# Softmax attention: a scheduling step that issues a transpose of probabilities before the next pair's scores

## The chip, the cores and the metric

The kernel runs on one core of a Trainium2 chip. TensorE multiplies matrices (its matmuls are "PE" in the profile, its weight loads "PEld"). VectorE (DVE) and ScalarE (ACT) do elementwise work, GpSimd (POOL) a few small operations, and SyncE (SP) issues the DMAs. Each engine takes its instructions in the order in which they stand for it, and waits on semaphores for the others. The metric is the device time of one execution in microseconds (us). The kernel before takes 996.15 us in the median of three runs (992.35, 996.15 and 997.11).

## The reference

256 tokens of width 1024 pass a first block (stick-breaking attention, pooling, spatial gating and an MLP), and then a second block of two layers, each with an MLP: a convolution layer, and an attention layer. The change is in the attention layer. The reference writes it as block-sparse attention with blocks of 256 keys; with 256 tokens there is one block, so that what is left is causal softmax attention with a distance penalty, in 16 heads of 64:

```
q, k, v = split(h @ w_qkv, 3)                     # 256 x 1024 each
q = rms_norm(to_heads(q), q_norm_g); k = rms_norm(to_heads(k), k_norm_g); v = to_heads(v)
s = einsum('bhqd,bhkd->bhqk', q, k) / sqrt(64) - slope[h] * (t_q - t_k)   # -inf where t_k > t_q
p = softmax(s, axis=-1)
y = einsum('bhqk,bhkd->bhqd', p, v) merged over heads @ w_o
x = x + g1 * y                                    # and then the MLP of this layer
```

All of it is fp32 to within the tolerance; a matrix product by weights is done in three fp32r products of high and low parts.

## The kernel before, in words

**Weights.** All weights stream through one list of 1 MB halves in the order of their use. A half is loaded by SP into one of three raw buffers, then split into a high part by ACT (`wH`, L352, two instructions a half) and a low part by DVE (`wL`, L353, two instructions), which go into one of four slots. A slot comes free when the product that reads it is done, and the split of a later half waits for that. So each product of the program releases splitting work on ACT and DVE.

**A job.** `ts_job` (L513) multiplies 128 tokens by 512 columns of weights: 24 matmuls of 128x512 (L446 to L448) into one PSUM bank of kind A. The attention layer has eight jobs for queries and keys (two halves `n` of the heads, two token tiles `t`, query and key), four jobs for the values, and four for the output matrix `ao`. Below, Q1 and K1 are the last two query and key jobs (`n`=1, `t`=1), V00, V01, V10, V11 the value jobs (`n`, `t`).

**Queries and keys.** After a query or key job, `qk_norm` (L1193) squares on ACT (L1196), sums by head on DVE (L1197), takes the power -1/2 on POOL (L1198, L1199) and multiplies on DVE (L1201). `qk_trans` (L1205) then transposes the 128x512 result by four PE transposes (L1210) into a bank of kind B, and ACT copies it out (L1211).

**Scores.** `at_scores(h0)` (L1216) handles the two heads h0 and h0+1, named S0, S2, ..., S14 below: matmuls into two B banks (L1224), and then for each head on DVE the penalty added (L1228), two maxima (L1230, L1231), on ACT two exponentials with their sums (L1232, L1233), and on DVE the reciprocal and two multiplications (L1234 to L1236). The probabilities stay in one of four buffers `w15`.

**Transposes of probabilities.** `at_trans(h)` (L1241), named T0 to T15, transposes the three 128x128 blocks of one head by PE into a B bank (L1245), and ACT copies them out (L1250).

**Value products.** `av(h)` (L1287), named W0, W2, ..., W14, multiplies two heads' transposed probabilities by the values (L1295, L1296); every second one splits a bank into the high and low parts that `ao` reads (L500, L501).

**What sets the order.** The program calls `at_step` at fixed places: two calls after each of the last three query and key jobs, three after each value job, then loops until the value products are done. A step issues the scores of a pair when at most two heads have scores that are not transposed yet (`state["s"] - state["t"] <= 2`), and a transpose when more than `AHEAD` = 2 heads are ahead, or when all scores up to the limit are issued. The order of the calls sets priorities. A scheduler then places each engine's instructions by them and by its own estimate of when inputs are ready, so that the order on an engine is near to, and not the same as, the order of the calls. There are four B banks, which scores and both kinds of transposes share.

Of the kernel before, what the change touches and what calls it, by code (L numbers as in the profile page):

```python
# [105 lines left out]
def net_kernel(ctx: ExitStack, tc: tile.TileContext, I, out):  # L106
# [8 lines left out]
    def nm(s):  # L115
        cnt[0] += 1
        return f"{s}_{cnt[0]}"
# [3 lines left out]
    def T(shape, tag, bufs, dt=F32):  # L121
        if tag in BASE_PAD and tag not in based:
            based.add(tag)
            sb.tile([P, BASE_PAD[tag]], F32, tag="pad" + tag, bufs=1, name=nm("pad"))
        return sb.tile(shape, dt, tag=tag, bufs=bufs, name=nm(tag))
# [4 lines left out]
    def bankB():  # L130
        return ps.tile([P, 512], F32, tag="B", name=nm("B"))
# [1084 lines left out]
    def at_scores(h0):  # L1216

        n, c = h0 // 8, (h0 % 8) // 2
        q, k = QK[0, n], QK[1, n]
        zs = [bankB(), bankB()]  # L1220
        for q0, q1, k1 in ((0, P, P), (P, S, S)):
            for i, z in enumerate(zs):
                po = slice(i * 64, i * 64 + 64)
                mm(z[:, q0:q0 + k1], q[po, c, q0:q1], k[po, c, 0:k1], start=True, stop=True)  # L1224
        for i, z in enumerate(zs):
            h = h0 + i
            s = wk.tile([P, 384], F32, tag="w15", bufs=4, name=nm("w15"))
            stt(s, dist, -slopes[h], z[:, :384], op0=ALU.mult, op1=ALU.add)  # L1228
            m = T([P, 2], "ss", 4)
            nc.vector.reduce_max(m[:, 0:1], s[:, 0:P], axis=AX.X, negate=True)  # L1230
            nc.vector.reduce_max(m[:, 1:2], s[:, P:384], axis=AX.X, negate=True)  # L1231
            act(s[:, 0:P], s[:, 0:P], AF.Exp, bias=m[:, 0:1], accum_out=sums[:, 0, h:h + 1])  # L1232
            act(s[:, P:384], s[:, P:384], AF.Exp, bias=m[:, 1:2], accum_out=sums[:, 1, h:h + 1])  # L1233
            nc.vector.reciprocal(sums[:, :, h:h + 1], sums[:, :, h:h + 1])  # L1234
            vts(s[:, 0:P], s[:, 0:P], sums[:, 0, h:h + 1], None, op0=ALU.mult)
            vts(s[:, P:384], s[:, P:384], sums[:, 1, h:h + 1], None, op0=ALU.mult)  # L1236
            stp[h] = s
# [3 lines left out]
    def at_trans(h):  # L1241
        s = stp.pop(h)
        pt = bankB()
        for i in range(3):
            nc.tensor.transpose(pt[:, i * P:(i + 1) * P], s[:, i * P:(i + 1) * P], ident)  # L1245
        if h % 2 == 0:
            tag, bufs = ("q4", 4) if 8 <= h < 12 else ("hidH" if h % 4 else "hidL", 2)
            ptt[h // 2] = T([P, 2, 384], tag, bufs)
        PT[h] = ptt[h // 2][:, h % 2, :]
        act(PT[h], pt[:, :384], AF.Copy)  # L1250

    state = {"s": 0, "t": 0, "o": 0}

    def at_step(lim):
        if state["s"] < lim and state["s"] - state["t"] <= 2:
            at_scores(state["s"])
            state["s"] += 2
        if state["t"] < state["s"] - AHEAD or (state["t"] < state["s"] and state["s"] >= lim):
            if state["t"] < 12 or state["o"] >= state["t"] - 10:
                at_trans(state["t"])  # L1260
                state["t"] += 1

    pend = []

# [4 lines left out]
    for n in range(2):  # L1269
        bq, bk = B["aq", n], B["ak", n]  # L1270
        need(bq, bk)
        for t in range(NT):
            for i, b in enumerate((bq, bk)):
                a = ts_job(hk, t, b)
                qn = qk_norm(a)
                if t == 1:
                    done(b)
                flush(HOLD)
                pend.append((n, t, i, qn))
                if n == 1 and t + i > 0:  # L1280
                    for _ in range(2):
                        at_step(8)
# [22 lines left out]
    for n in range(2):  # L1305
        need(B["av", n])
        for t in range(NT):
            a = ts_job(hk, t, B["av", n])
            if t == 1:
                done(B["av", n])  # L1310
            act(vt[t][:, n * 512:(n + 1) * 512], a, AF.Copy)
            flush()
            for _ in range(3):
                at_step(16)
                if n == 1:
                    av_next(8)
    while state["o"] < 8:
        at_step(16)
        av_next(8)
# [45 lines left out]
```

## Time and profile before

| what | value |
|---|---|
| median of three runs | 996.15 us (992.35 to 997.11) |
| the profiled execution's own time | 997.19 us |
| its span | 995.5 us |
| PE busy | 967.3 us, 97% of the span, 4969 matmuls |
| DVE, ACT, POOL busy | 75%, 57%, 6% |
| granted TensorE clock, mean | 0.997 |
| attention, from the first scores to the start of `ao` | 722.8 to 786.3 us |
| mean DMA rate | 224 GB/s |

An engine is busy while it executes instructions; the ends of matmuls are modelled, so that PE's 97% says where PE had work and not how well it was used. The granted clock is 1.00 at TensorE's full 2.4 GHz and 0.50 at 1.2 GHz. In the timeline, a note in brackets gives the engine's idle time ahead of the instruction and what ended it.

### The profile page before, as it was taken

Reading aid. Unit: us, or ns where it says so; the run is one execution under the profiler, and the core shown is the slowest. Engines: PE = TensorE matmul, PEld = TensorE weight load, DVE = VectorE, ACT = ScalarE, POOL = GpSimd, SP = SyncE. Lnnn points to the kernel's source line nnn. Section 1 sums busy time; section 2 is a strip of 40 time slices with the busy share of each in tenths; the row PEclk is TensorE's granted clock in tenths of the full one; section 3 lists DMA queues with packets and bytes.
Section 4 is the critical chain, followed back from the end, with each engine's and each line's share of the span. In section 5 each row is a group of like instructions: output and inputs, shape, how many; then the busy total and the mean of one; then the engine's idle time right before and its main releaser. Section 6 shows DMA issues by size and latency. Waiting matters only on the chain.

```text
span 995.5 us, 13007 instructions
## 1 busy us (share of the span) xinstructions
PE 967.3 (97%) x4969; PEld 798.1 (80%) x4969; DVE 743.9 (75%) x1036; ACT 564.0 (57%) x872; POOL 59.2 (6%) x84
## 2 busy tenths in 40 slices
PE   7999999988999999999999999999999999999998
PEld 5998889877788887875778888888866778888886
DVE  6858887787587887989788678869578586766553
ACT  5656784456466556523556666555477456656561
POOL 4002010010000000100000000000420000000000
PEclk9999999999999999999999999999999999999999
DMA  7877686577667986678269777865534246567531
GB/s 249 278 275 258 233 285 239 186 248 258 236 224 263 311 297 228 213 266 274 84 217 311 270 258 253 306 247 198 176 121 170 85 143 238 212 241 255 201 128 43
DMA packets 102044, 223.38 MB, mean 224 GB/s; under 512 B 4316, under 2 KB 8310, under 8 KB 101982
## 3 DMA queue, kind: packets, MB, share of 16 engines
q1 hardware_dynamic: 101982, 222.55, 64.8%
q8 instruction: 39, 0.64, 0.3%
q14 instruction: 23, 0.19, 0.1%
HBM read 221.44 MB, written 1.10 MB: 224 GB/s over the span
## 4 chain that ended last, share of the span: by engine, by line
PE 74%; DVE 13%; DMA 4%; ACT 3%; issue 3%; POOL 2%; POOLq 0%; SPq 0%; ACTq 0%; DVEq 0%
PE B L461 14%; PE A L448 12%; PE A L447 12%; PE A L446 12%; PE B L462 7%; DVE wL L353 5%; PE A L461 4%; DMA raw<-in_ada_w_dram 2%; PE A L462 2%; ACT wH L352 2%; DVE acc L372 2%; POOL rst L531 2%; PE A L453 1%; PE A L454 1%; PE A L455 1%
## 5 line engine op out<-in xcount | busy, mean ns | idle before, releaser
L353 DVE TENSOR_TENSOR wL<-raw,wH 128x1024 fp32r<-128x1024 f32 x306 | 361.9, 1220 | 82.6 <-ACT wH L352 81.5
L352 ACT ACTIVATE wH<-raw 128x1024 fp32r<-128x1024 f32 x306 | 307.2, 1050 | 153.5 <-PE A L448 97.4
L461 PE MATMUL B<-hHL,wH 128*128 128x512 f32 x576 | 205.2, 400 | 0.0
L462 PE MATMUL B<-hHL,wL 128*128 128x256 f32 x576 | 162.3, 282 | 0.0
L446 PE MATMUL A<-wH,hidH 128*128 128x512 f32 x384 | 151.3, 394 | 0.0
L447 PE MATMUL A<-wL,hidH 128*128 128x512 f32 x384 | 150.5, 392 | 0.0
L448 PE MATMUL A<-wH,hidL 128*128 128x512 f32 x384 | 150.3, 391 | 0.0
L372 DVE SCALAR_TENSOR_TENSOR acc<-raw,cond,acc 128x512 f32<-128x512 f32 x168 | 125.7, 748 | 13.0 <-DMA raw<-in_ada_w_dram 10.2
L446 PE MATMUL A<-wH,hHL 128*128 128x512 f32 (+1 forms) x336 | 130.4, 388 | 1.5 <-ACT wH L352 0.8
L461 PEld LDWEIGHTS B<-hHL,wH 128*128 128x128 f32 x576 | 109.0, 189 | 26.9
L447 PE MATMUL A<-wL,hHL 128*128 128x512 f32 (+1 forms) x336 | 129.1, 384 | 0.5 <-DVE wL L353 0.5
L448 PE MATMUL A<-wH,hHL 128*128 128x512 f32 (+1 forms) x336 | 128.9, 384 | 0.0
L462 PEld LDWEIGHTS B<-hHL,wL 128*128 128x128 f32 x576 | 109.4, 190 | 0.8
L446 PEld LDWEIGHTS A<-wH,hidH 128*128 128x128 f32 x384 | 72.4, 189 | 16.0 <-issue 0.8
L448 PEld LDWEIGHTS A<-wH,hidL 128*128 128x128 f32 x384 | 72.5, 189 | 15.6
L447 PEld LDWEIGHTS A<-wL,hidH 128*128 128x128 f32 x384 | 72.6, 189 | 14.7
L446 PEld LDWEIGHTS A<-wH,hHL 128*128 128x128 f32 x336 | 63.7, 190 | 15.1 <-issue 1.3
L447 PEld LDWEIGHTS A<-wL,hHL 128*128 128x128 f32 x336 | 63.6, 189 | 13.0 <-DVE wL L353 1.0
L448 PEld LDWEIGHTS A<-wH,hHL 128*128 128x128 f32 x336 | 63.5, 189 | 12.5 <-issue 0.3
L461 PE MATMUL A<-hHL,wH 128*128 128x512 f32 x192 | 68.2, 398 | 0.0
L968 ACT ACTIVATE rs<-B 128x256 f32<-128x256 f32 x72 | 27.1, 376 | 50.5 <-PE B L462 50.4
L531 POOL TENSOR_TENSOR rst<-rst,neghalf 128x1 f32<-128x1 f32 x20 | 18.4, 923 | 625.5 <-DVE rst L528 560.8
(242 smaller groups left out, 1269.2 us busy)
## 6 DMA issues: line engine op xcount, KB each, us to landing
raw<-in_mlp_w_dram SPq DMA_DIRECT2D x64, 1024.0 KB
raw<-in_ada_w_dram SPq DMA_DIRECT2D x48, 1024.0 KB
raw<-in_w_in_dram SPq DMA_DIRECT2D x19, 1024.0 KB
raw<-in_w_ff_in_dram SPq DMA_DIRECT2D x16, 1024.0 KB
raw<-in_w_ff_out_dram SPq DMA_DIRECT2D x16, 1024.0 KB
raw<-in_attn_w_qkv_dram SPq DMA_DIRECT2D x12, 1024.0 KB
raw<-in_conv_w_in_dram SPq DMA_DIRECT2D x8, 1024.0 KB
ada<-mod SPq DMA_DIRECT2D x24, 256.0 KB
```

Of the source, the lines that this page charges most:

```text
L352: act(h[:, p:q, :], v[:, p:q, :], AF.Copy)
L353: nc.vector.tensor_sub(l[:, p:q, :], v[:, p:q, :], h[:, p:q, :].bitcast(F32))
L372: stt(acc_cur[0], v[:, c, :], cond[:, k:k + 1], src, op0=ALU.mult, op1=ALU.add)
L446: mm(dst, lh(xc), wh, start=s0, stop=False)
L447: mm(dst, lh(xc), wl, start=False, stop=False)
L448: mm(dst, ll(xc), wh, start=False, stop=s1)
L453: mm(dst, wh, rh(xc), start=(i == 0), stop=False)
L454: mm(dst, wh, rl(xc), start=False, stop=False)
L461: mm(dst, wh, km.HL[:, :, k, :], start=(k == 0), stop=False)
L462: mm(dst[:, 0:S], wl, km.HL[:, 0, k, :], start=False, stop=(k == KC - 1))
L531: nc.gpsimd.tensor_tensor(rs, rs, neg_half, op=ALU.pow)
L968: act(r1[:, s, :], a[:, S:2 * S], AF.Copy)
```

## The change

```diff
     def at_step(lim):
-        if state["s"] < lim and state["s"] - state["t"] <= 2:
-            at_scores(state["s"])
-            state["s"] += 2
+        new = state["s"] < lim and state["s"] - state["t"] <= 2
         if state["t"] < state["s"] - AHEAD or (state["t"] < state["s"] and state["s"] >= lim):
             if state["t"] < 12 or state["o"] >= state["t"] - 10:
                 at_trans(state["t"])
                 state["t"] += 1
+        if new:
+            at_scores(state["s"])
+            state["s"] += 2
```

Whether a pair is due is still decided at the start of a step, but its scores are issued after the transpose. The test for the transpose now sees the old `state["s"]`, so that in a step where two heads wait it finds 2 > 2 false and leaves the transpose to a later step. By the calls alone the steps run as follows (a bracket is a step):

```
before: (S0) (S2 T0) | Q1 (T1) (S4 T2) | K1 (T3) (S6 T4) | V00 (T5) (S8 T6) (T7) | V01 (S10 T8) (T9) (S12 T10)
        | V10 (T11) W0 (S14 T12) W2 (T13) W4 | V11 (T14) W6 (T15) () | W8 W10 W12 W14
now:    (S0) (S2) | Q1 (T0) (T1) | K1 (S4) (T2) | V00 (T3) (S6) (T4) | V01 (T5) (S8) (T6)
        | V10 (T7) W0 (S10) W2 (T8) W4 | V11 (T9) W6 (S12) (T10) | (T11) W8 (S14) W10 (T12) (T13) W12 (T14) (T15) W14
```

No operation is added or removed; 16 heads' work is spread otherwise. The lines behind the change stand one lower in the new file (L1295 is L1296, L1311 is L1312).

Three places show it engine by engine. In the rows, `A_...` and `B_...` are PSUM banks, `w_...` the probabilities of a head, `rs_...` a normalised query or key, `q_...`, `hidL_...` and `hidH_...` tiles that hold queries, keys or transposed probabilities, `gb_...` the values, `wH_...` and `wL_...` the split weights.

PE from the end of V00 (bank A_6592 before) to the start of V01 (A_6672), before:

```order
L1210 MATMUL B_6618<-ident_69,rs_6435 128x128 x4
L1210 MATMUL B_6624<-ident_69,rs_6528 128x128 x4
L1245 MATMUL B_6630<-ident_69,w_1093_6481 128x128 x3
L1224 MATMUL B_6635<-q_1107_6546,q_1086_6453 128x128
L1224 MATMUL B_6636<-q_1107_6546,q_1086_6453 128x128
L446 MATMUL A_6672<-wH_6437,hHL_5952 128x512
L1224 MATMUL B_6635<-q_1107_6546,q_1086_6453 128x256
L1224 MATMUL B_6636<-q_1107_6546,q_1086_6453 128x256
```

The same place now (V00 is A_6555, V01 is A_6630):

```order
L1210 MATMUL B_6581<-ident_69,rs_6429 128x128 x4
L1210 MATMUL B_6587<-ident_69,rs_6496 128x128 x4
L1245 MATMUL B_6593<-ident_69,w_1072_6388 128x128 x3
L1224 MATMUL B_6598<-q_1050_6261,q_1038_6205 128x128
L1224 MATMUL B_6598<-q_1050_6261,q_1038_6205 128x256
L446 MATMUL A_6630<-wH_6431,hHL_5952 128x512
L1224 MATMUL B_6599<-q_1050_6261,q_1038_6205 128x128
L1224 MATMUL B_6599<-q_1050_6261,q_1038_6205 128x256
L1245 MATMUL B_6624<-ident_69,w_1103_6527 128x128 x3
```

Here stood T5 and S8; now T3, S6 and T4 stand here, behind the same two transposes of normalised queries and keys (those of Q1 and K1).

DVE at this place, before (the sums of K1's squares are `ssq_6522`, its product `rs_6528`):

```order
L1197 TENSOR_REDUCE ssq_6522<-junk_6523 128x8
L353 TENSOR_TENSOR wL_6531<-raw_6259,wH_6530 128x1024
L1234 RECIPROCAL sums_6089<-sums_6089 128x2 x2
L1201 TENSOR_TENSOR rs_6528<-A_6497,ssq_6522 128x512
L1235 TENSOR_SCALAR w_1091_6471<-w_1091_6471,sums_6089 128x128
...
L353 TENSOR_TENSOR wL_6531<-raw_6259,wH_6530 128x1024
```

DVE at this place now (K1's are `ssq_6490` and `rs_6496`, the heads of S4 are `w_1103` and `w_1105`):

```order
L353 TENSOR_TENSOR wL_6499<-raw_6259,wH_6498 128x1024 x2
L1197 TENSOR_REDUCE ssq_6490<-junk_6491 128x8
L1228 SCALAR_TENSOR_TENSOR w_1103_6527<-cst_6080,B_6521 128x384
L1201 TENSOR_TENSOR rs_6496<-A_6465,ssq_6490 128x512
L353 TENSOR_TENSOR wL_6507<-raw_6437,wH_6506 128x1024 x2
L1230 TENSOR_REDUCE ss_6529<-w_1103_6527 128x1
L1231 TENSOR_REDUCE ss_6529<-w_1103_6527 128x1
L1228 SCALAR_TENSOR_TENSOR w_1105_6537<-cst_6080,B_6522 128x384
```

Two splits more stand ahead of K1's sums, and two stand between the first head of S4 and its maxima.

DVE behind V11, now (the splits are of the second half of `ao`'s columns; the heads of S12 are `w_1164` and `w_1166`, those of S14 `w_1174` and `w_1176`):

```order
L353 TENSOR_TENSOR wL_6825<-raw_6661,wH_6824 128x1024 x2
L1228 SCALAR_TENSOR_TENSOR w_1164_6850<-cst_6080,B_6844 128x384
L501 TENSOR_TENSOR ok_6777<-A_6786,ok_6776 128x512
...
L1228 SCALAR_TENSOR_TENSOR w_1166_6860<-cst_6080,B_6845 128x384
L1228 SCALAR_TENSOR_TENSOR w_1174_6892<-cst_6080,B_6886 128x384
...
L1228 SCALAR_TENSOR_TENSOR w_1176_6902<-cst_6080,B_6887 128x384
...
L1236 TENSOR_SCALAR w_1176_6902<-w_1176_6902,sums_6089 128x256
L501 TENSOR_TENSOR q_1179_6917<-A_6931,q_1178_6916 128x512
```

Before, the last two heads' multiplications stood ahead of those splits; now the whole softmax of four heads stands behind them. On PE the same place now reads, from T10 on:

```order
L1245 MATMUL B_6870<-ident_69,w_1144_6751 128x128 x3
L1296 MATMUL A_6881<-q_1152_6784,gb_6553 64x256
L1245 MATMUL B_6876<-ident_69,w_1146_6761 128x128 x3
L1297 MATMUL A_6881<-q_1152_6784,gb_6554 64x128
...
L1245 MATMUL B_6942<-ident_69,w_1176_6902 128x128 x2
L1297 MATMUL A_6931<-hidH_6940,gb_6554 64x128
L448 MATMUL A_6959<-wH_6655,ok_6777 128x512
...
L1297 MATMUL A_6931<-hidH_6940,gb_6554 64x128
```

T11 to T15, the four last value products and both last pairs of scores now stand behind V11, seven matmuls of the first `ao` job (A_6959) among them, and transposes stand between the matmuls of the value products W8, W12 and W14.

## Rows read from the trace of the kernel before

**Rows 1.** The page: span, and busy time by engine.
```profile
span 995.5 us, 13007 instructions
PE 967.3 (97%) x4969; PEld 798.1 (80%) x4969; DVE 743.9 (75%) x1036; ACT 564.0 (57%) x872; POOL 59.2 (6%) x84
```

**Rows 2.** Busy by stretch: PE, PEld, DVE, ACT, POOL; granted clock, DMA share, GB/s.
```profile
722.80:775.20 52.40, 47.74 (x268) 34.83 (x267) 42.50 (x110) 38.02 (x99) 7.51 (x6) 1.00 0.37 130
...
820.00:990.00 170.00, 170.00 (x843) 143.22 (x842) 101.30 (x120) 93.79 (x131) 0.00 (x0) 1.00 0.55 192
```

**Rows 3.** Timeline of PE in attention: start, length, instruction, count, idle before.
```profile
723.89 1.36 PE L1224 MATMUL B<-q,q 64*128 64x256 f32 x10
...
730.94 0.61 PE L1245 MATMUL B<-ident,w 128*128 128x128 f32 x3 [1.84 <-DVE w L1235]
...
748.47 0.61 PE L1245 MATMUL B<-ident,w 128*128 128x128 f32 x3 [1.49 <-DVE w L1235]
...
771.73 0.93 PE L1224 MATMUL B<-q,q 64*128 64x128 f32 x8
...
775.15 0.50 PE L446 MATMUL A<-wH,hHL 128*128 128x512 f32 x1
...
780.77 0.49 PE L1245 MATMUL B<-ident,w 128*128 128x128 f32 x3
781.19 0.66 PE L1295 MATMUL A<-hidH,gb 128*64 128x256 f32 x4
...
782.00 0.55 PE L1245 MATMUL B<-ident,w 128*128 128x128 f32 x3
```

**Rows 4.** Timeline of DVE in attention.
```profile
719.32 0.68 DVE L1197 TENSOR_REDUCE ssq<-junk 128x8 f32<-128x512 f32 x1
722.11 0.69 DVE L1201 TENSOR_TENSOR rs<-A,ssq 128x512 f32<-128x512 f32 x1 [2.11 <-POOL ssq L1199]
...
735.21 0.68 DVE L1197 TENSOR_REDUCE ssq<-junk 128x8 f32<-128x512 f32 x1
...
738.90 0.69 DVE L1201 TENSOR_TENSOR rs<-A,ssq 128x512 f32<-128x512 f32 x1 [1.88 <-POOL ssq L1199]
739.51 2.35 DVE L353 TENSOR_TENSOR wL<-raw,wH 128x1024 fp32r<-128x1024 f32 x2
...
772.68 1.02 DVE L1228 SCALAR_TENSOR_TENSOR w<-cst,B 128x384 f32<-128x384 f32 x2 [0.73 <-PE B L1224]
...
776.24 0.35 DVE L1236 TENSOR_SCALAR w<-w,sums 128x256 f32<-128x256 f32 x1
...
782.11 2.36 DVE L353 TENSOR_TENSOR wL<-raw,wH 128x1024 fp32r<-128x1024 f32 x2 [0.36 <-ACT wH L352]
...
792.09 0.69 DVE L574 TENSOR_TENSOR rs<-A,ada 128x512 f32<-128x512 f32 x1 [4.35 <-PE A L448]
```

**Rows 5.** Timeline of ACT in attention.
```profile
752.15 1.26 ACT L1211 ACTIVATE q<-B,cols 128x512 f32<-128x512 f32 x2
...
773.93 0.40 ACT L1232 ACTIVATE w<-w,ss 128x128 f32<-128x128 f32 x1 [0.22 <-DVE ss L1230]
...
774.83 0.39 ACT L1232 ACTIVATE w<-w,ss 128x128 f32<-128x128 f32 x1
...
784.25 0.50 ACT L1250 ACTIVATE hidH<-B 128x384 f32<-128x384 f32 x1
```

**Rows 6.** Timeline of POOL in attention.
```profile
723.90 0.24 POOL L1198 TENSOR_SCALAR ssq<-ssq 128x8 f32<-128x8 f32 x1 [1.83 <-DVE ssq L1197]
...
735.98 1.14 POOL L1198 TENSOR_SCALAR ssq<-ssq 128x8 f32<-128x8 f32 x1 [10.10 <-DVE ssq L1197]
```

**Rows 7.** Busy time by stretch, with the granted clock, around 245 us.
```profile
240.00:245.00 5.00, 2.35 (x10) 1.51 (x9) 3.87 (x6) 1.01 (x2) 0.00 (x0) 1.00 0.87 324
245.20:248.60 3.40, 3.20 (x10) 2.72 (x11) 3.15 (x5) 2.96 (x4) 0.00 (x0) 0.50 0.93 298
...
262.30:265.70 3.40, 3.40 (x8) 2.69 (x9) 3.35 (x5) 2.52 (x6) 0.00 (x0) 0.50 0.96 378
```

## The prediction

> **What bounds the kernel now.** I read the page first, then the busy time by stretch, then the timeline of PE, DVE, ACT and POOL through attention. PE is busy for 97% of the span and DVE for 75% [rows 1], so the reader should look for the places where PE has nothing to do. In the MLP behind attention PE is busy for 170.00 of 170.00 us [rows 2]: whatever attention loses or wins there goes to the end. In attention, from the first scores to the last value job, PE is idle for 52.40 - 47.74 = 4.66 us, while DVE and ACT are busy for 42.50 and 38.02 us [rows 2]. PE waits there for the softmax: 1.84 us ahead of T0 and 1.49 us ahead of T5, both times for a multiplication on DVE [rows 3]. Neither DVE nor ACT is full, but they work in a fixed order, in which the splits of weights stand among the softmax. So what the change is worth hangs on which wait comes last at each place of the new order, and I walk along that order with durations from the rows.
>
> **Prices.** A job is 24 matmuls from 775.15 to 780.77 us, 5.62 us or 0.234 each; three transposes of a head go from 780.77 to 781.19, 0.42 us, or 0.14 a transpose; the value products of a pair take 0.81 us, from 781.19 to 782.00 [rows 3]. A pair's scores take 0.93 us, half of them 0.45 [rows 3]. Four transposes of a query or key, at 0.14, are 0.56 us. On DVE two splits are 2.3 us, a penalty 0.5, two maxima 0.5 (ACT starts on the first head at 773.93, 0.23 behind the two penalties, which is the first, smaller maximum) [rows 4, 5]. On ACT the two exponentials of a head take 0.9 us (773.93 to 774.83), a transposed query or key 0.63, a transposed head 0.50 [rows 5].
>
> **Up to V00, a gain.** The first scores end at 725.25 in both orders [rows 3]. Before, 16 matmuls of Q1 followed and then T0, which waited. Now 23 matmuls (5.4) and the transposes of a query (0.56) come first: T0 is reached at 731.2, and was ready at 730.94, so that its 1.84 us go, because other work covers them. T0, T1 (0.84), K1 (5.62), transposes (0.56), S4 (0.93), T2 (0.42) and V00 (5.62) bring PE to 745.2.
>
> **Between V00 and V01, three new waits.** PE does the transposes of Q1 (0.56, to 745.8). The next are those of K1, which need K1's normalised product on DVE. There the product of Q1 is at 738.90 as before, since the exponentials and splits ahead of it have not moved; then stand four splits (739.5 to 744.1) where there were two, the sum of squares, and the product. From that sum to the product it took 2.79 us (719.32 to 722.11) and 3.69 us (735.21 to 738.90) [rows 4]. The difference is POOL's first operation, 0.24 us in the first case and 1.14 in the second, when a split ran on DVE [rows 6]. Now a penalty that reads a PSUM bank stands there instead, so I take 2.79, and keep 0.9 more as the upper bound: the product comes at 746.9, PE goes on at 747.7. That is a wait of 1.9 us.
>
> The Trainium skill, page "SBUF — State Buffer", section "SBUF: two separate sides", says that VectorE and GpSimd share a pair of ports, which a VectorE operation with two SBUF inputs holds against a GpSimd one until it ends. The rows on POOL agree with it (a split has two SBUF inputs), and by it the wait is the 1.9 us taken; without it, 2.8 us and a sum 0.9 us higher.
>
> Behind this wait on PE stand T3 (to 748.7) and S6. S6's first bank is one that S4's second penalty has to free, and on DVE two splits (747.5 to 749.8), two maxima and that penalty come first, to 750.8: a second wait of 2.2 us. Its second bank is freed by ACT's copy of Q1's transposes, which stands behind the exponentials of both heads of S4 and the copy of V00: from 750.1, 0.9 + 0.5 + 0.9 + 0.63 gives 753.0, a third wait of 1.4 us. Then half of S6 and T4, and V01 starts at 754.0. So 5.5 us of waits stand here, where before T5's 1.49 stood.
>
> **V01 to V11.** 23 matmuls (5.4), T5, S8, T6 (1.8), V10 (5.62), T7, W0, S10, W2, T8, W4 (4.2) and V11 (5.62) end at 776.6. I see no wait in this part, as each transpose's softmax was issued a job earlier. Before, V11 ended at 780.77 [rows 3], so at this point the new order is 4.2 us ahead, but with five more transposes and two pairs of scores (3.9 us) still to do.
>
> **Behind V11, a loss.** Before, T14, T15 and five value products went with hardly a wait, and `ao` started 5.5 us after V11. Now the softmax of four heads has to run in that time. On DVE it stands behind two splits that V11's end releases: before, those ran until 784.5, 3.7 us behind V11's end [rows 4], so now until 780.3. The softmax of one pair took DVE from 772.68 to 776.59, 3.9 us with short waits for ACT [rows 4]. Two pairs are 7.8 us, and two bank splits of 0.6 between them make 9.0; since one pair's waits are filled by the other I take 8.2, which ends at 788.5. The last head then needs two transposes (0.3), the copy (0.50) [rows 5], its half of the products (0.4), and 0.8 for three passes between engines and two matmuls of `ao` that stand in between: 790.5. Seven of `ao`'s first 24 matmuls are done by then, 17 are left (4.0): its first job ends at 794.5. Before, DVE took that job's result at 792.09 [rows 4]. That is 2.4 us later. The value products W8 and W12, which transposes now part in the middle, may lose the overlap of their two heads (four passes of them ran in 0.66 us [rows 3]), 0 to 0.4 us each; they stand where PE waits for DVE anyway, so I take 0.3 in all, and 0.3 of POOL's 0.9.
>
> **Sum.** +2.4 + 0.3 + 0.3 = +3.0 us. The profiled execution took 997.19 us by itself, so it would be 1000.2; it is 1.04 us above the median of 996.15. On the median the sum gives 999.2 us. Later stages keep the order they had, and their DMAs are issued by the same releases, so nothing there gives it back: DMA's share was 0.37 in attention [rows 2].
>
> **Rivals.**
> *Faster: the new waits are covered.* DVE is idle for 9.9 of 52.4 us [rows 2]. If the normalised key and the banks are there in time, the second and third wait between V00 and V01 (3.6 us) go, and if the softmax of S12 and S14 keeps pace, PE needs only its 8.8 us behind V11 and starts `ao` 1 us earlier than before. That is -1.0 to -4.6, in the middle -2.8 us: 993.4. Against it: the splits stand ahead in DVE's own order, and nothing lets it pass them. Chance 0.14.
> *Slower: the clock falls.* In 240 to 245 us PE was busy for 2.35 of 5 us; from 245.2 the granted clock was 0.50, which is 1.2 GHz, for 3.4 us, and again from 262.3 [rows 7]. There 10 and 8 matmuls ran where 3.4 / 0.234 = 14.5 fit: 10.9 matmuls or 2.6 us lost. Attention's waits of up to 1.84 us did not do this: the clock stayed at 1.00 [rows 2]. The new place has 5.5 us of waits in 8.2 us. If the clock falls as it did there, the sum is +5.6: 1001.8. It decides from idle time like that at 242 us. Chance 0.20.
> The Trainium skill, page "TensorE: Matmul & The Clock Gate", section "HAM oscillation — how this bites in real kernels", says that idle gaps between bursts of matmuls bring the half clock back, and advises against them; the rows at 245 us agree.
> *Slower: the end is longer.* If the two pairs' softmax does not overlap (9.0, not 8.2) and `ao`'s seven early matmuls wait too (1.6), the sum is +5.4: 1001.5. For it speaks that ACT's copies stand between the exponentials; against it, that these matmuls need only banks that were split long before. Chance 0.08.
> The forecast has the remaining 0.58, with a range of its own from +0.5 to +5 us, 996.7 to 1001.2.
>
> **Numbers.** 0.5% is 5.0 us, about what a measurement tells from no change. Slower by more: 0.05 of the forecast's chance, 0.18 of the clock's, 0.07 of the longer end's, together 0.30. Faster by more: 0.05 of the covered waits'. Within: 0.65. The range leaves out most of the covered waits and the far end of the clock: 995.0 to 1003.3 us.
>
> **What would show it.** Each step has its mark in the new trace: no idle time ahead of T0; idle PE ahead of K1's transposes for DVE (L1201), and ahead of both banks of S6, about 5.5 us in all, with V01 starting near 754; V11 ending some 4 us earlier than 780.77; two splits on DVE right behind V11 and the softmax of S12 behind them; the first `ao` job done 2 to 3 us later than before. The granted clock is to stay at 1.00 through attention. It is wrong if V01 starts before 751, if `ao`'s first job ends before 792, if a stretch at 0.50 follows, or if a stage behind attention shortens.

## The result, and the profile after

The changed kernel takes 1002.75 us in the median (1000.91 to 1004.42), the kernel before on the same chip 994.29: a ratio of 1.0086, with a 95% interval of 1.0069 to 1.0103, so 8.5 us slower. In the trace the loss lies in attention alone:

| from | before | after | difference |
|---|---|---|---|
| second half of the first scores (723.89 and 721.68 us) to the end of V11 | 56.88 | 55.47 | -1.4 |
| end of V11 to DVE's taking `ao`'s first job (L574) | 11.32 | 20.31 | +9.0 |
| sum | 68.2 | 75.8 | +7.6 |
| L574 to the end of the span | 203.4 | 203.4 | 0.0 |

Ahead of attention the changed trace is 2.2 us earlier, with the same instructions. Times are therefore compared from the row of the first scores on: 2.21 us are to be added to a time of the trace after to compare it with [rows 3, 4].

The page after, which answers to [rows 1], has the same work in a longer span:

```profile
span 1000.9 us, 13008 instructions
PE 972.2 (97%) x4969; PEld 800.9 (80%) x4969; DVE 744.1 (74%) x1036; ACT 564.1 (56%) x872; POOL 58.4 (6%) x84
```

Busy time by stretch after (the stretch, its length, then the columns of [rows 2]; the first number behind the five engines is the granted clock):

```profile
721.68:743.19 21.51, 21.43 (x111) 16.97 (x110) 16.48 (x35) 15.83 (x32) 5.57 (x6) 1.00 0.27 89
743.19:747.25 4.06, 0.96 (x8) 0.75 (x7) 2.99 (x4) 0.00 (x0) 1.04 (x1) 1.00 0.82 310
747.26:757.49 10.23, 9.23 (x23) 6.46 (x24) 6.31 (x23) 6.21 (x21) 0.00 (x0) 0.50 0.30 104
757.50:777.20 19.70, 19.70 (x114) 15.04 (x113) 13.47 (x31) 12.84 (x29) 0.00 (x0) 1.00 0.33 108
777.20:797.46 20.26, 17.86 (x103) 11.16 (x102) 11.40 (x31) 10.87 (x29) 0.00 (x0) 1.00 0.30 104
```

The second row is the new place of waits: PE busy for 0.96 of 4.06 us. Right behind it the clock stands at 0.50, which is 1.2 GHz, for 10.2 us. In the last row PE is idle for 2.4 us, and works in small pieces, as the timeline shows.

PE after, at the places of [rows 3]:

```profile
728.75 1.28 PE L1245 MATMUL B<-ident,w 128*128 128x128 f32 x6
...
745.10 0.63 PE L1210 MATMUL B<-ident,rs 128*128 128x128 f32 x4 [1.91 <-DVE rs L1201]
745.57 0.49 PE L1245 MATMUL B<-ident,w 128*128 128x128 f32 x3
748.26 1.65 PE L1224 MATMUL B<-q,q 64*128 64x128 f32 x4 [2.20 <-DVE w L1228]
749.84 0.79 PE L446 MATMUL A<-wH,hHL 128*128 128x512 f32 x1
750.56 1.65 PE L1224 MATMUL B<-q,q 64*128 64x128 f32 x4
752.14 0.90 PE L1245 MATMUL B<-ident,w 128*128 128x128 f32 x3
752.69 0.77 PE L447 MATMUL A<-wL,hHL 128*128 128x512 f32 x1
...
753.69 0.63 PE L446 MATMUL A<-wH,hHL 128*128 128x512 f32 x1
...
754.97 0.63 PE L446 MATMUL A<-wH,hHL 128*128 128x512 f32 x1
...
783.96 0.61 PE L1245 MATMUL B<-ident,w 128*128 128x128 f32 x3 [0.63 <-DVE w L1235]
786.34 0.65 PE L1296 MATMUL A<-hidL,gb 128*64 128x256 f32 x2 [1.77 <-ACT hidL L1250]
...
790.06 0.40 PE L447 MATMUL A<-wL,ok 128*128 128x512 f32 x1
790.29 0.27 PE L1245 MATMUL B<-ident,w 128*128 128x128 f32 x1
...
792.94 0.38 PE L1297 MATMUL A<-hidH,gb 128*64 128x128 f32 x2
```

T0 and T1 go without a wait at 728.75. The forecast waits of 1.9 and 2.2 us are there as 1.91 and 2.20, with the releasers named in advance. The two halves of S6 then run at half clock, and so do the first matmuls of V01: three of them take 1.28 us (753.69 to 754.97), where three at full clock take 0.70. At the end, the last head's transposes start at 790.29, behind matmuls of `ao`.

DVE after, which answers to [rows 4], and POOL, which answers to [rows 6]:

```profile
741.47 0.68 DVE L1197 TENSOR_REDUCE ssq<-junk 128x8 f32<-128x512 f32 x1
744.26 0.69 DVE L1201 TENSOR_TENSOR rs<-A,ssq 128x512 f32<-128x512 f32 x1 [1.65 <-POOL ssq L1199]
744.87 2.35 DVE L353 TENSOR_TENSOR wL<-raw,wH 128x1024 fp32r<-128x1024 f32 x2
...
778.49 2.36 DVE L353 TENSOR_TENSOR wL<-raw,wH 128x1024 fp32r<-128x1024 f32 x2 [0.36 <-ACT wH L352]
780.77 0.55 DVE L1228 SCALAR_TENSOR_TENSOR w<-cst,B 128x384 f32<-128x384 f32 x1
...
788.91 0.35 DVE L1236 TENSOR_SCALAR w<-w,sums 128x256 f32<-128x256 f32 x1
...
797.46 0.69 DVE L574 TENSOR_TENSOR rs<-A,ada 128x512 f32<-128x512 f32 x1 [2.77 <-PE A L448]
```

```profile
733.40 1.14 POOL L1198 TENSOR_SCALAR ssq<-ssq 128x8 f32<-128x8 f32 x1 [9.74 <-DVE ssq L1197]
...
742.24 0.24 POOL L1198 TENSOR_SCALAR ssq<-ssq 128x8 f32<-128x8 f32 x1 [5.95 <-DVE ssq L1197]
```

From K1's sum to its product it is 2.79 us, as taken. The splits behind V11 (777.15 us) end 3.7 us later, and S12 stands behind them. The last softmax ends at 789.26.

One thing follows from the code alone. With the old count in both tests, a step that issues scores needs at most two waiting heads, and one that issues a transpose needs more than two: no step does both. With the two parts of the changed step swapped back, and the old count kept in both tests, the program would make the same calls in the same order. So the change is not "a transpose first"; it is one operation a step where there were two.

### The profile page after: what moved, and what is told of

It is laid out like the page before. It is cut to its first block, busy times and chain, and to the rows that moved or that the text cites. A ratio compares the mean times of both kernels' runs of the same rounds, so it can differ in the third digit from the quotient of the medians.

```text
span 1000.9 us, 13008 instructions
## 1 busy us (share of the span) xinstructions
PE 972.2 (97%) x4969; PEld 800.9 (80%) x4969; DVE 744.1 (74%) x1036; ACT 564.1 (56%) x872; POOL 58.4 (6%) x84
## 4 chain that ended last, share of the span: by engine, by line
PE 76%; DVE 12%; DMA 3%; ACT 3%; issue 3%; POOL 2%; POOLq 0%; SPq 0%; ACTq 0%; DVEq 0%
PE B L461 14%; PE A L448 13%; PE A L447 12%; PE A L446 12%; PE B L462 7%; DVE wL L353 5%; PE A L461 4%; PE A L462 2%; POOL rst L531 1%; PE A L453 1%; ACT wH L352 1%; PE A L454 1%; PE A L455 1%; DMA raw<-in_ada_w_dram 1%; DMA raw<-in_w_in_dram 1%
## 5 line engine op out<-in xcount | busy, mean ns | idle before, releaser
L447 PEld LDWEIGHTS A<-wL,hidH 128*128 128x128 f32 x384 | 72.2, 188 | 14.5
```

The source lines that it names most:

```text
L447: mm(dst, lh(xc), wl, start=False, stop=False)
```

## The experiments

All times are against the kernel before on the same chip. "To V11" and "behind" are the two parts of the first table, in us of the profiled execution; "at 0.50" are the stretches between 700 and 800 us.

| run | to V11 | behind | sum | at 0.50 | median, ratio and 95% interval |
|---|---|---|---|---|---|
| before | 56.9 | 11.3 | 68.2 | none | |
| after | 55.5 | 20.3 | 75.8 | 10.2 | 1002.75, 1.0086 (1.0069 to 1.0103) |
| e1_fill | 52.3 | 21.8 | 74.1 | 3.4 | 1000.94, 1.0062 (1.0045 to 1.0080) |
| e2_mid | 57.4 | 13.6 | 71.0 | 6.8 | 995.98, 1.0020 (1.0004 to 1.0036) |
| e3_tail | 53.9 | 15.0 | 68.9 | none | 994.20, 1.0001 (0.9987 to 1.0016) |
| e4_retest | 56.6 | 11.3 | 67.9 | none | 994.64, 1.0007 (0.9993 to 1.0021) |
| e5_order | 56.5 | 11.4 | 67.9 | none | 993.48, 0.9997 (0.9981 to 1.0014) |
| e6_more | 57.3 | 10.9 | 68.2 | none | 995.16, 1.0003 (0.9987 to 1.0019) |
| e7_noearly | 54.0 | 22.5 | 76.5 | 6.8 + 3.4 | 1002.43, 1.0091 (1.0059 to 1.0123) |
| e8_late | 58.1 | 11.3 | 69.4 | 3.4 | 995.34, 1.0007 (0.9992 to 1.0022) |
| e9_tail2 | 52.3 | 18.5 | 70.8 | none | 997.29, 1.0029 (1.0015 to 1.0044) |
| e10_mid2 | 61.7 | 10.2 | 71.9 | 10.2 | 999.44, 1.0047 (1.0029 to 1.0066) |
| e11_bank | 53.0 | 21.7 | 74.7 | 6.8 + 3.4 | 1000.81, 1.0058 (1.0039 to 1.0077) |
| e12_retest_bank | 56.3 | 11.3 | 67.6 | 3.4 | 994.83, 0.9998 (0.9981 to 1.0014) |

**e1_fill: the clock by itself.**

```diff
+    def fill(pt, k):
+        for _ in range(k):
+            mm(pt, hk.H[0][:, 0, 0:P], hk.HL[:, 0, 0:2, :].rearrange("p a b -> p (a b)"), start=True, stop=True)
...
+        if (n, t, i) == (1, 1, 1):
+            fill(pt, 8)
...
+        if h == 3:
+            fill(pt, 9)
```

> The changed kernel, with 17 matmuls of 128x512 added whose results are overwritten: 8 ahead of the transposes of K1 and 9 ahead of T3, where PE was idle for 1.91 and 2.20 us and where the clock fell to 0.50 at 747.3 us for 10.2 us. They take 17 x 0.23 = 3.9 us, the place of the idle time. Theory (the fall of the clock costs what V11's end came too late, 779.4 in the frame of the kernel before against 776.6 forecast): the clock stays at 1.00, V11 ends 2.8 us earlier, and the time is 1002.75 - 2.8 = 1000.0 us, 5.7 above the kernel before. Rival (the softmax behind the waits sets V01 and what follows, so that PE loses nothing by its clock): the clock stays at 1.00 and the time at 1002.8, 8.5 above before. Second rival (idle time is not what lowers the clock): it falls here too, and the time is 1002.8 or more.

PE and the clock in that place (L1207 are the added matmuls), and behind V11:

```profile
742.92 2.10 PE L1207 MATMUL B<-hHL 128*128 128x512 f32 x8
744.98 0.66 PE L1216 MATMUL B<-ident,rs 128*128 128x128 f32 x4
745.39 2.31 PE L1207 MATMUL B<-hHL 128*128 128x512 f32 x9
747.54 0.49 PE L1253 MATMUL B<-ident,w 128*128 128x128 f32 x3
...
750.40 0.92 PE L1230 MATMUL B<-q,q 64*128 64x128 f32 x6 [1.68 <-ACT q L1217]
```

```profile
743.10:748.70 5.60, 5.39 (x27) 3.92 (x25) 4.43 (x9) 1.27 (x5) 1.10 (x1) 1.00 0.67 231
748.70:774.00 25.30, 23.62 (x134) 18.15 (x134) 18.31 (x49) 17.78 (x46) 0.00 (x0) 1.00 0.35 124
...
783.67:787.07 3.40, 3.40 (x12) 1.97 (x12) 1.44 (x6) 1.94 (x6) 0.00 (x0) 0.50 0.00 0
```

With PE busy the clock stays at 1.00 and V11 ends 3.1 us earlier, where 2.8 were expected. At full clock the third wait shows too: 1.68 us for ACT's copy, forecast as 1.4. Of the 3.1 us the sum kept 1.7 (75.8 to 74.1), since the clock now fell behind V11, where the changed kernel has the same two waits without a fall, and that part is 1.5 us longer. The intervals of the two times overlap, so the reading rests on the traces: the fall in the middle costs 3.1 us, and with the idle PE time filled it did not come; the rival that PE loses nothing by it is out. e7 below, with the same order and the same two waits in the middle, had 6.8 us at 0.50 and reached V11's end at 54.0, between the two.

**e2_mid and e3_tail: one part of the order each.** The new step stands in the first branch, the old one in the second; e3_tail has 16 in the place of 8.

```diff
     def at_step(lim):
+        if lim == 8:
...
+        else:
...
```

> The new step is used for the query and key jobs alone (limit 8), the old step behind them. The place between V00 and V01 keeps the waits of the changed kernel; behind V11 stands the softmax of S14, no longer that of S12. Theory (a loss by the fallen clock at V00, and a loss for each pair whose softmax stands behind V11): V11 ends 0.8 us later than before (2.2 us of work more ahead of it than in the changed kernel), and behind it two splits (3.7), one pair's softmax (3.9), the last head (2 to 4) and 4.1 to the end of ao's first job make 13.7 to 15.7 us against 11.3: +3.2 to +5.2, 997.5 to 999.5 us, clock at 0.50 for about 10 us near 747. Rival (the middle costs all of it): 1002.8. Rival (the tail costs all, the middle nothing): +2 to +4 at most, 996 to 998, with V11 ending no later than before.

> The old step for the query and key jobs (limit 8), the new step behind them. Between V00 and V01 the order is that of the kernel before; behind V11 stands the softmax of S14. Theory (as for the run with the new step in the first part alone): no fall of the clock at V00; V11 ends 2.2 us earlier than before, as S14 and three heads' transposes stand behind it; then 13.7 to 15.7 us to the end of ao's first job: +0.2 to +2.2, 994.5 to 996.5 us. Rival (the tail costs all 8.5 us, half of it for each pair): +4, 998.5. Rival (the middle costs all): 994.3 or less.

In the traces e2 loses 2.8 us (13.6 behind V11, the low end of what was expected) and e3 0.7, as expected. Both times miss their ranges at the low end: e2 took 995.98 us for 997.5 to 999.5, and its executions differ in the clock, from 995.1 us at a mean of 0.997 to 1001.3 at 0.990; e3 took 994.20 for 994.5 to 996.5, which lies with the rival that the middle costs all. So these two runs do not decide between the places. By the ratios the two halves together cost 2.1 of 8.5 us. Each has one pair's softmax behind V11, where the changed kernel has two, and this leaves open what the second pair costs.

**e9_tail2 and e10_mid2: the whole tail, and the whole middle.** e9 is e3 with S12 held until V11 (in the new step):

```diff
-        new = state["s"] < lim and state["s"] - state["t"] <= 2
+        new = state["s"] < lim and state["s"] - state["t"] <= 2 and (state["s"] < 12 or "v11" in state)
```

e10 is e2 with four calls after each value job, which bring S12 and S14 ahead of V11:

```diff
-            for _ in range(3):
+            for _ in range(4):
                 at_step(16)
```

> The old step for the query and key jobs, the new step behind them, with S12 held back until V11 has been issued. The middle is that of the kernel before, and behind V11 stands the softmax of S12 and S14, as in the changed kernel. Theory (the changed kernel's 7.6 us between the first scores and the end of ao's first job are 3.1 of clock in the middle and 4.5 behind V11): V11 ends 52.4 us behind the first scores, two splits, two pairs' softmax and the last head follow as in the changed kernel (20 us, where 20.5 stood there and 11.5 before), in all 72.4, 4.3 more than before, clock at 1.00 through the middle: 998 to 999 us. Rival (one pair behind V11 costs nothing, and a second one little): 0 to +2, 994 to 996. Rival (the two pairs cost all of it): +7 or more, 1001 us.

> The new step for the query and key jobs, the old step behind them with four calls after each value job, so that S14 too stands ahead of V11. The middle is that of the changed kernel up to T4, with its two waits; the tail is that of the kernel before, with T14 and T15 earlier. Theory (the middle costs what its clock costs): with a fall of 6.8 to 10.2 us at V00 +1.5 to +2.2, 996 to 996.5 us; in an execution without a fall there -1. Rival (the middle costs nothing, the tail all): -1 to 0. Rival (the middle costs more than its clock): +4 or more, 998 us.

```profile
723.16:775.50 52.34, 47.83 (x256) 36.33 (x255) 38.65 (x92) 35.42 (x83) 7.52 (x6) 1.00 0.35 122
775.50:793.98 18.48, 16.95 (x100) 11.71 (x100) 11.51 (x30) 10.49 (x28) 0.00 (x0) 1.00 0.34 113
```

```profile
744.95:747.00 2.05, 0.12 (x1) 0.15 (x2) 0.96 (x2) 0.00 (x0) 1.05 (x1) 1.00 1.02 384
747.02:757.25 10.23, 8.68 (x32) 5.56 (x31) 7.79 (x23) 6.59 (x22) 0.00 (x0) 0.50 0.41 148
```

The first fence is e9 up to and behind V11: a full clock, and a tail of 18.5 us where before had 11.3; in all +2.6 us (997.29 us for 998 to 999), less than the 4.3 expected, because its tail is 1.8 us shorter than the changed kernel's. The second is e10 in the middle: the same fall of 10.2 us. It costs +3.7 us in the trace and 4.7 by the time, more than the 1.5 to 2.2 expected, so the time lies with the rival that the middle costs more than its clock. The rows put most of the cost down to the clock all the same. PE was busy for 8.68 us at half clock; with the 1.28 us for 0.70 above, an estimate of what this lost is 3.9 us, and PE's idle time up to V11 is 0.9 us less than before (3.8 for 4.7): together 3.0 of the 3.7. S6 also stands in two parts there, as in the changed kernel and as S4 in e4 below; whether that is the rest the run does not show. By the times, middle and tail are 4.7 and 2.9 us (0.47% and 0.29% of 994.3), together 7.6 of the 8.5; in the traces 3.7 and 2.6 of 7.6. So the loss stands in two places, and the first is the larger by both measures. The shares are rough, since neither run has the changed kernel's middle or tail exactly.

**e5_order and e6_more: is it the order in a step, or the number of operations?**

In e5 the transpose is tested with the count that it will have:

```diff
+        due = state["s"] + 2 if new else state["s"]
-        if state["t"] < state["s"] - AHEAD or (state["t"] < state["s"] and state["s"] >= lim):
+        if state["t"] < state["s"] and (state["t"] < due - AHEAD or due >= lim):
```

In e6 each place has one call more (four where there were three):

```diff
-                    for _ in range(2):
+                    for _ in range(3):
                         at_step(8)
```

> The transpose stands ahead of the scores in a step, and which of both a step does is tested as in the kernel before, so that the steps hold what they held (T0 with S2, T2 with S4, and so on) in the other order. Theory (what costs is that the changed steps do one thing each, so that two pairs' softmax comes to stand behind V11; the order within a step is worth little): S12 and S14 stay ahead of V11, the first scores of a pair start 0.4 us (three transposes) later, some pairs have their two banks parted on PE (0.86 us a bank, where both together take 0.93: +0.8 for each such pair, some two pairs), the waits ahead of T0 and T5 stay: 0 to +2, 994 to 996 us, clock at 1.00 from 700 to 800 us. Rival (the transpose ahead of the scores is itself the loss): +5 or more, 999 us and above.

> The changed step, called once more at each place (three times after a query or key job, four after a value job). A step still does one thing, but there are enough of them: S12 and S14 stand ahead of V11 again, T0 behind S2 as before. Theory (too few steps are the cause): the loss goes but for what T15 and the value products behind V11 cost: -0.5 to +1, 993.3 to 995 us, no fall of the clock between 740 and 800 us. Rival (one operation a step costs by its order): 998 us or more.

Within their intervals both came out as their first theory said: ratios of 0.9997 and 1.0003, no fall in attention, and for e6 a sum of 68.2 us, that of the kernel before. A transpose ahead of the scores costs nothing when the step still does both, and one operation a step costs nothing when there are enough steps.

**e4_retest, e8_late and e12_retest_bank: can the saved waits be kept?** e4 makes the test for scores behind the transpose:

```diff
-        new = state["s"] < lim and state["s"] - state["t"] <= 2
...
-        if new:
+        if state["s"] < lim and state["s"] - state["t"] <= 2:
```

e8 is the kernel before with T0 and T4 left to a call that stands behind the next job:

```diff
             state["s"] += 2
+            if state["t"] in (0, 4):
+                return
...
+    def at_late():
+        if state["t"] in (0, 4) and state["t"] < state["s"] - AHEAD:
+            at_trans(state["t"])
+            state["t"] += 1
```

e12 is e4 with another bank for each pair's second head:

```diff
-        zs = [bankB(), bankB()]
+        zs = [bankB(), bankA()]
```

> The transpose stands first in a step, and the test for the next pair is made after it (with the new count) and not ahead of it. Each step can again do both. T0 stands behind Q1, S4 behind T1, S14 ahead of V11, as the last pair. Theory (the loss comes from steps that do one thing where they did two, and not from the transpose that stands first): the waits ahead of T0 (1.84) and T5 (1.49) go, as 24 and more matmuls cover them, no new one comes, and no pair's softmax stands behind V11: -1 to -3.3, 991 to 993.3 us. Rival (a transpose ahead of the scores delays the softmax, and that is the loss): 998 to 1003 us, with waits between V00 and V01 as in the changed kernel.

> The kernel before, with T0 issued behind Q1 and T4 behind V00 (ahead of the transposes of the normalised queries), and nothing else moved: the two transposes that waited for 1.84 and 1.49 us in the middle of a job. Theory (waits of a transpose that stands inside a job can be covered by the rest of that job, as T0's was in the changed kernel, when nothing else is delayed with it): both waits go, no pair's scores come later: -1.5 to -3.3 us, 990.5 to 992.3. Rival (what PE saves there it waits for at the next pair's banks, which these transposes and the copies behind them hold): -0.5 to +1, 993.3 to 995.

> The kernel with the test for the next pair made after the transpose (measured 0.25 us less than before from the first scores to the end of ao's first job), with the second bank of each pair's scores taken from the A banks. There PE waited 1.10 us for a bank ahead of S4's second half, and the halves of S4 and S6 stood apart on PE (4 records in 0.92 us each, where both halves together take 0.93 for 8). Theory (the two are what used up the 3 us of waits ahead of T0 and T5 that this order saves): the bank wait goes and both pairs stand together: 1.1 + 0.9 + 0.9 = 2.9 us less, at least half of it kept against new waits for DVE: -1.5 to -3 against the kernel before, 991 to 993 us. Rival (DVE sets the sum of the waits: what is saved here is waited for at the next transposes): -0.5 to +0.5.

PE in e4, at S4:

```profile
727.72 0.92 PE L1224 MATMUL B<-q,q 64*128 64x128 f32 x4
...
733.16 0.92 PE L1224 MATMUL B<-q,q 64*128 64x128 f32 x4 [1.10 <-ACT q L1211]
```

PE in e8, at S4 and at K1's transposes:

```profile
734.21 0.92 PE L1224 MATMUL B<-q,q 64*128 64x128 f32 x6 [1.36 <-ACT hidL L1250]
...
752.54 0.66 PE L1210 MATMUL B<-ident,rs 128*128 128x128 f32 x4 [2.31 <-DVE w L1228]
```

PE in e12, at S6:

```profile
741.66 0.37 PE L1224 MATMUL B<-q,q 64*128 64x128 f32 x1 [2.13 <-DVE w L1228]
```

The clock behind these waits, in e8 and in e12:

```profile
754.31:757.71 3.40, 3.40 (x9) 2.20 (x7) 1.32 (x6) 1.68 (x6) 0.00 (x0) 0.50 0.67 257
```

```profile
743.04:746.44 3.40, 3.40 (x9) 2.64 (x9) 1.94 (x5) 3.40 (x9) 2.56 (x2) 0.50 0.74 280
```

e4's theory on the loss held, its gain did not come: 1.84 and 1.49 us of waits went, and waits of 1.10 for a bank and 1.26 for DVE ahead of T4 came, with halves of S4 and S6 that stand apart. In e8 the idle time of PE between the first scores and `ao` is 4.67 us, the same as before: 1.36 us for a copy by ACT and 2.31 for DVE stand at two new places. In e12 the bank wait and the parted halves are gone, and 2.13 us stand ahead of S6. By the times the rivals were right in both. In e8 it is as its rival said: what PE no longer waits for at one transpose it waits for at the next bank or result. In e12 the idle time up to V11 is 1.0 us less than before (3.65), and the sum 0.6 us less; that it is not more goes in part to 3.4 us at half clock behind the wait of 2.13 (nine matmuls in them, where 14.5 fit at 0.234: an estimate of 1.3 us). None of them beats the kernel before; all three intervals hold 1.

**e7_noearly: the last head.** The jobs of `ao` take their last two chunks first.

```diff
-                res[t, n] = ts_job(km, t, b, bias=bias[n])
+                res[t, n] = ts_job(km, t, b, bias=bias[n], kcs=K8[6:] + K8[:6] if km is ok_km[0] else None)
```

> The changed kernel, in which the jobs of ao take the chunks of heads 12 to 15 first, so that no matmul of ao can stand on PE ahead of the last value product. In the changed kernel eight did, four of them ahead of T15, and the last value product ended 4.0 us behind the last softmax (789.26 to 793.26) where 2.0 were forecast. Theory (those matmuls took the place of the last head): the last value product now ends 2.0 to 2.3 us behind the last softmax, 24 matmuls (5.6) and the split (1.4) follow, and ao's first job ends 1 us later than in the changed kernel: 1003 to 1004 us. Rival (the last head waits for ACT and DVE and not for PE): still 4.0 us, and ao's first job ends 3 us later: 1005.5 us.

```profile
785.44 0.35 DVE L1238 TENSOR_SCALAR w<-w,sums 128x256 f32<-128x256 f32 x1
...
795.51 0.69 DVE L574 TENSOR_TENSOR rs<-A,ada 128x512 f32<-128x512 f32 x1 [5.56 <-PE A L448]
```

```profile
788.21 0.38 PE L1300 MATMUL A<-hidH,gb 128*64 128x128 f32 x2
```

The last value product now ends at 788.59, 2.8 us behind the last softmax (785.79), not 4.0; 2.0 to 2.3 were expected. So `ao`'s early matmuls took 1.2 us of the 2.0 that the last head was late. Without them the sum is 0.7 us longer (1 expected), but its stretches at 0.50 differ from those of the changed kernel. From the last softmax to `ao`'s first result, where both run at full clock, it is 9.7 us (785.79 to 795.51) for 8.2 (789.26 to 797.46); 0.69 us of the 9.7 are a new wait of PE for the split. The changed kernel has seven of `ao`'s matmuls done by the last value product, and not the eight of the expectation: they are worth more than the delay that they cause.

**e11_bank: the bank, or DVE?** The changed kernel with e12's bank:

```diff
-        zs = [bankB(), bankB()]
+        zs = [bankB(), bankA()]
```

> The changed kernel, with the second bank of each pair's scores taken from the four A banks (jobs and value products use them) and not from the four B banks. In the changed kernel S6 waited 2.20 us for a bank and its two banks were parted; now both its banks are free in time, and T4 behind it waits for the probabilities of S4 (ready at about 749.3 us in that trace) instead. Theory (PE's waits between V00 and V01 are set by DVE, whatever stands in front): idle time of 1.9 us ahead of K1's transposes stays, about 1.9 stands ahead of T4 in place of the 2.20, S6 is done in between (0.93 and no third wait): V01 starts about 2 us earlier at full clock; with the clock's fall the gain is 2, without it 5: 998 to 1001 us. Rival (the bank was the cause of the loss in the middle): no wait behind K1's transposes, no fall, -6 or more: 996.5 or less.

```profile
745.30 0.63 PE L1210 MATMUL B<-ident,rs 128*128 128x128 f32 x4 [1.91 <-DVE rs L1201]
...
750.62 0.90 PE L1245 MATMUL B<-ident,w 128*128 128x128 f32 x3 [3.09 <-ACT q L1211]
```

```profile
746.57:753.38 6.81, 3.72 (x14) 2.59 (x13) 6.08 (x21) 5.69 (x20) 0.00 (x0) 0.50 0.47 160
```

S6 no longer waits, and T4 behind it waits for 3.09 us (1.9 expected), for a bank again. The time lies in the range of the theory. Its two cases, with a fall and without, may be what sets the executions apart: two with a mean clock of 0.998 took 996.84 and 996.85 us, the eight at 0.991 to 0.996 took 999.23 to 1004.85; the mean is that of the whole execution and does not say where the clock fell. The bank alone was not the cause: K1's transposes still wait for 1.91 us for DVE, and the time stays 0.58% above before.

## Why the prediction was right or wrong

The time lies in the range, near its upper end, and the direction is right. That it lies in the range is in part luck: the range was laid around 996.15 us, the median of three runs, and the kernel before is at 994.29 in six; around that the same changes would end at 1001.4. The size is not right: +3.0 us were forecast, +7.6 stand in the trace, and the 8.5 of the times lie in the class that had a chance of 0.30.

- **Up to V00, a gain:** right. No wait ahead of T0.
- **Between V00 and V01:** right in its three waits: 1.91, 2.20, and 1.68 at full clock (e1), for 1.9, 2.2 and 1.4. POOL's operation took 0.24 us beside a penalty that reads PSUM and 1.14 beside a split, so the lower bound held. The Trainium skill, page "SBUF — State Buffer", section "SBUF: two separate sides", says that a VectorE operation with two SBUF inputs holds the ports that it shares with GpSimd against a GpSimd operation; these rows agree. V01's matmuls, but for one, begin at 752.69, which is 754.9 in the time of the trace before, for 754.0.
- **V01 to V11:** this is the step that failed. "The granted clock is to stay at 1.00 through attention": it was 0.50 for 10.2 us, and V11 ended 1.4 us ahead of before and not 4.2. In e1, at full clock, it ended 4.5 us ahead. The mechanism was the second rival, with a chance of 0.20 and a price of 2.6; it measured 3.1. (The sum behind that price gives 11.1 matmuls, not 10.9, which leaves it at 2.6.) I had argued from single waits of up to 1.84 us that left the clock alone, but at this place two follow each other with 0.96 us of work in 4.06. The Trainium skill, page "TensorE: Matmul & The Clock Gate", section "HAM oscillation — how this bites in real kernels", says that idle gaps between bursts of matmuls bring the half clock back. The rows agree in that, but the waits on DMA that the section tells of are longer than the 1.91 and 2.20 us that did it here.
- **Behind V11:** the splits (3.7 us) and the softmax of two pairs (8.5 us, for 8.2) are right. The mis-sized term is the last head: 2.0 us were taken, 4.0 measured. Its transposes stood behind four matmuls of `ao`, and its product behind two more; the rows of the order showed that `ao` matmuls stand in between, and I had counted two. e7 gives 1.2 us of it back to that cause; the rest I cannot divide among the parted value products and the passes between engines.
- **Sum:** 2.4 forecast up to `ao`'s first job, 2.8 that V11 came too late, 0.2 for the splits and the softmax together, 2.0 for the last head and 0.2 behind it make 7.6. Of the two allowances of 0.3, POOL's did not come (2.79 us, as taken); that for the parted value products can't be told apart from the rest.
- **Marks:** the stretch at 0.50 is one that was named as showing the forecast wrong. `ao`'s first job came 7.6 us later, not 2 to 3. No later stage gave anything back: 203.4 us in both.

## What to carry to other kernels

When a step of a schedule may issue two operations and a condition makes it one, count how many operations are then left behind the last point where they were covered; the order within the step is the smaller matter. Where a change makes waits of PE longer or puts two next to each other, price the half clock behind them as part of the forecast and not as an exception, and look for it in the granted clock first. A wait of PE for DVE or ACT can move when a transpose is moved, as in e8, so the sum of the waits is to be compared, not the one that went.

## What the runs showed of the hardware

Idle PE time of the same size does not always lower the clock. The changed kernel's waits of 0.63 and 1.77 us behind V11 left it at 1.00, the same two in e7 and nearly the same in e1 (0.62 and 1.77) were followed by 3.4 us at 0.50. Nor were two waits needed: in e8 one of 2.31 us, in e12 one of 2.13, were followed by 3.4 us at 0.50, and in e11 the clock was down from 746.57, after the wait of 1.91 us and ahead of that of 3.09. The wait of 1.84 us ahead of T0 in the kernel before was not. Ahead of attention, where these kernels issue the same instructions, the row of the first scores starts at 718.0 us in e6, with no stretch at 0.50, and at 724.0 in e8, with two of 3.4 us; e3 and e4, with none either, are at 719.4, so that the clock is not all of it. This is why the table counts from that row.

The scores of two heads, which use 64 rows of the array each, overlap: both halves of a pair take 0.93 us for eight records [rows 3], and in e4 each half alone takes 0.92 for four. A pair whose banks do not come free together costs 0.9 us more.
